# Delta rule on one Trainium2 core: projections from tokens with both norms applied, and other due times

## The chip, the core and the metric

The kernel runs on one core of one Trainium2 chip. The core has four engines that compute, each with its own queue of instructions: TensorE (PE, matrix products, with PEld its weight loads), VectorE (DVE), ScalarE (ACT) and GpSimd (POOL). SyncE (SP) and the others also start DMA transfers. The engines wait for each other through semaphores. PE writes to PSUM, from where DVE or ACT takes the result to SBUF (an "eviction"). The metric is the device time of one execution in microseconds.

## The reference, cut to what matters

Two blocks run one after the other on 512 tokens of width 1024. The first ends in a final RMS norm; the second has a delta-rule layer, a feed-forward layer, a stick-breaking attention and another feed-forward layer. The change lies in the delta-rule layer:

```
x  = first_block(...)                       # its last step: rms_norm with final_norm_g
hn = rms_norm(x, attn_norm)                 # a second norm
proj = hn @ w_in                            # q, k, v, z, b, a
qkv = silu(causal_depthwise_conv(qkv, conv_w))   # four taps along the tokens
q, k = l2_norm(heads(q)), l2_norm(heads(k)); v = heads(v)
beta = sigmoid(b); g = -exp(a_log) * softplus(a + dt_bias)
o = gated_delta_rule(q, k, v, beta, g)      # chunks, a triangular solve each, a scan
out = (rms_norm(o, o_gain) * silu(z)) @ w_out
```

## The kernel before

Activations stand feature by token: a tile of 128 x 512 holds 128 features of all tokens, and eight of them (k = 0 to 7) hold a token's 1024. Each product is made of three matmuls in a rounded format: tokens and weights are each split into a high part (a rounding copy by ACT) and a low part (a subtraction by DVE or POOL). In the traces ah and al are the parts of the tokens, whi and wlo those of the weights, wraw the weights as they come from DRAM, and mm is the PSUM tile of a product. `mm3` issues the three matmuls of 128 x 512.

The order of the instructions of every engine is set when the kernel is built. The code runs through a planner that keeps an estimated clock for each engine. The main line issues the matmuls of the projections; beside it stand "lanes", queues of Python generators with the side products (convolutions, norms, the solve and so on). After each `mm3`, `tick` (line 452) lets a lane take its next step if its due time has come by PE's estimated clock. A generator gives up at each `yield`; `yield 1.5` sets the next step due 1.5 us later than it would be. So due times and changed costs move instructions in the order, and not only in time. Nearly every instruction is recorded at one line, L232, so the rows are told apart by the names of their tiles.

The delta-rule stage is `gdn`. `head`, ahead of it, ends the first block and makes the first projection (key gk, heads 0 and 1) from tokens x * fag, where fag is the product of the two norms' gains; the norms themselves need sums over all 1024 features that are complete only later. `gdn` then makes Rc, the product of both norms' factors for each token (128 x 512, the same on all partitions). Since a factor for each token can be multiplied in behind a projection as well as ahead of it, each projection's PSUM tile is multiplied by Rc as it is evicted.

The projections come in the order `GDN_ORDER`: k0, ba (the columns of beta and g), k1, k2, k3, q0, v0, q1, v1, q2, v2, q3, v3, z0 to z3. `fm_pair` issues one of them: two tiles m = 0, 1, each of eight k, in two halves of the weights, 48 matmuls in all, and calls `ev` for each tile. The steps behind a projection are:

- `conv` evicts to xm: a memset of three columns for the tokens ahead of the first, then `xm = ps * Rc` on DVE. `conv_gen` makes the four taps: ACT multiplies by the last tap's weight, DVE adds three taps (tiles kF, qF or vf, `stt`), ACT applies Silu.
- `norm_gen`, for q and k: ACT squares to cs, PE sums it with ones into the PSUM tile lC, DVE takes that to kss or qss. `v_gen`, for v: PE transposes vf into lC.
- `gates_gen`: from baf (the evicted ba) come beta, then gm, whose parts gmh and gml go to PE (lC<-gm with constants cst, later lB<-ub,gmh).
- `lower` (lB, XTs), DMAs through a scratch tensor scr, then `solve`: thirty pairs of DVE instructions sub and mt, one after the other, which invert the small triangular blocks; then `levels`, `prep`, `scan`, `o_norm` and `fin`, which multiplies with zs.
- z: DVE makes zy = ps * Rc, ACT applies Silu into zs.

Of the kernel before, what the change touches and what calls it, by code (L numbers as in the profile page):

```python
# [12 lines left out]
F = mybir.dt.float32  # L13
FR = mybir.dt.float32r
I32 = mybir.dt.int32
AF = mybir.ActivationFunctionType
OP = mybir.AluOpType
# [3 lines left out]
P = 128  # L21
T = 512
D = 1024
KT = 8
# [76 lines left out]
class Clock:  # L101
# [24 lines left out]
    def tile(s, x):  # L126

        r = s.tiles.get(x.name)
        if r is None:
            r = s.tiles[x.name] = [[], [], 0.0, 0.0]  # L130
            tag = getattr(x, "cap_key", None)
            if tag is not None and x.tag_meta is not None:
                ring = s.rings.setdefault(str(tag), [])
                ring.append(r)
                if len(ring) > x.tag_meta.bufs:
                    r[2] = ring.pop(0)[3]
        return r
# [245 lines left out]
class Kern:  # L383
# [1315 lines left out]
    def gdn(s):  # L1699
        nc, A = s.nc, s.A  # L1700
        V, S, G, PE = nc.vector, nc.scalar, nc.gpsimd, nc.tensor
        tt, stt = V.tensor_tensor, V.scalar_tensor_tensor
# [9 lines left out]
        hh, hl, st1, st2, first = s.begun  # L1712
# [7 lines left out]
        with s.aside():  # L1720
            s.rsqrt_(R1, p1, 1.0 / D)
            tt(out=Rc, in0=R1, in1=R1, op=OP.mult)
            tt(out=Rc, in0=p2, in1=Rc, op=OP.mult)
            s.rsqrt_(Rc, Rc, 1.0 / D)
            tt(out=Rc, in0=Rc, in1=R1, op=OP.mult)

        def scale_gen():
            for k in range(KT):
# [36 lines left out]
        def gates_gen(baf):  # L1765
            ps = bankC([4, 16])
            for t in range(4):
                PE.transpose(ps[:, t], baf[:, t * P:(t + 1) * P], s.ident[0:16, 0:16])
            yield
            S.activation(beta, ps[:, :, 0:8], AF.Exp, scale=-1.0)  # L1770
            V.tensor_scalar(out=beta, in0=beta, scalar1=1.0, scalar2=None, op0=OP.add)
            V.reciprocal(beta, beta)
            tt(out=gm, in0=ps[:, :, 8:16], in1=ab[:, None, 1].to_broadcast([P, 4, 8]), op=OP.add)
            S.activation(gex, gm, AF.Abs)
            S.activation(gex, gex, AF.Exp, scale=-1.0)
            S.activation(gex, gex, AF.Ln, bias=1.0)
            stt(out=gm, in0=gm, scalar=0.0, in1=gex, op0=OP.max, op1=OP.add)
            S.activation(ab[:, 0], ab[:, 0], AF.Exp)
            stt(out=gm, in0=gm, scalar=-1.0, in1=ab[:, None, 0].to_broadcast([P, 4, 8]),
                op0=OP.mult, op1=OP.mult)  # L1780
            s.split(gmh, gml, gm)
            yield
            ps = bankC([4, 32])
            gf = gm.rearrange("p t h -> p (t h)")
            for i, off in enumerate((C_UB, C_CB, C_C0, C_C1)):
                PE.matmul(ps[:, i], s.c[:, off:off + P], gf, start=i == 0, stop=i == 3, skip_group_check=True)
            yield
            V.tensor_copy(gc.rearrange("p t h -> p (t h)"), ps[:, 0])
            tt(out=kds.rearrange("p t h -> p (t h)"), in0=ps[:, 1], in1=gc.rearrange("p t h -> p (t h)"),
               op=OP.subtract)  # L1790
            S.activation(egl.rearrange("p c t h -> p c (t h)"), ps[:, 2:4], AF.Exp)
            S.activation(kds, kds, AF.Exp)
            S.activation(sc1, gc, AF.Exp)
            tt(out=sc1, in0=sc1, in1=beta, op=OP.mult)
            done.add("gates")
            yield

        def conv(ps, m):

            if len(s.lanes["V"]) + len(s.lanes["W"]) > 2:  # L1800
                s.until(lambda: len(s.lanes["V"]) + len(s.lanes["W"]) <= 2)
            xm = tile("xm", [T + 3], bufs=3)
            V.memset(xm[:, 0:3], 0.0)
            tt(out=xm[:, 3:], in0=ps, in1=Rc, op=OP.mult)
            return xm

        def conv_gen(xm, m, y, then):
            w = lambda j: s.vcol("conv_w", 24 * j + m)
            if y is None:
                yield from wait(("v", m - 18))  # L1810
                y = s.tp.tile([P, 512], F, name="vf", tag="nacc", bufs=2)
            S.activation(y, xm[:, 3:], AF.Copy, scale=w(3))
            for j in range(3):
                yield
                stt(out=y, in0=xm[:, j:j + T], scalar=w(j), in1=y, op0=OP.mult, op1=OP.add)
            yield
            S.activation(y, y, AF.Silu)
            yield
            s.add(then(y), "C")


# [1 line left out]
        def norm_gen(x, h, ss):  # L1823
            q = tile("cs", [512])
            S.activation(q, x, AF.Square)
            yield
            p = bankC([4, 2])
            for t in range(4):
                for c in range(2):

                    o = 64 * c if ss is kss else 64 - 64 * c
                    PE.matmul(p[o:o + 64, t], q[:, t * P + 64 * c:t * P + 64 * c + 64], s.ones[:, 0:2],
                              start=t == 0, stop=t == 3, skip_group_check=True)
            yield
            V.tensor_scalar(out=ss[:, :, h], in0=p[:, :, 0], scalar1=EPS, scalar2=None, op0=OP.add)
            if ss is kss:
                done.add(("kss", h))
            hs = slice(h // 4 * 4, h // 4 * 4 + 4)
            if ss is kss and all(("kss", i) in done for i in range(hs.start, hs.stop)):
                S.activation(rho[:, :, hs], kss[:, :, hs], AF.Ln)  # L1840
                S.activation(rho[:, :, hs], rho[:, :, hs], AF.Exp, scale=-0.5)
                V.reciprocal(kss[:, :, hs], kss[:, :, hs])
                tt(out=rho[:, :, hs], in0=rho[:, :, hs], in1=beta[:, :, hs], op=OP.mult)
                yield from wait("gates")
                stt(out=nbeta[:, :, hs], in0=kss[:, :, hs], scalar=-1.0, in1=beta[:, :, hs], op0=OP.mult,
                    op1=OP.mult)
                tt(out=sc1[:, :, hs], in0=sc1[:, :, hs], in1=kss[:, :, hs], op=OP.mult)
                done.add(("k", h // 4))
            if ss is qss:
                V.tensor_scalar(out=ss[:, :, h], in0=ss[:, :, h], scalar1=EPS * P, scalar2=None, op0=OP.mult)  # L1850
                done.add(("q", h))
            yield
# [259 lines left out]
        for key, _, j in s.GDN_ORDER:  # L2112
            if key == "ba":
                beta_and_g()
                continue
            if key == "gk" and j == 1:
                s.add(scale_gen(), "X")
            if key == "gq" and j == 0:
                s.until(lambda: "xd" in done)
                qs.append(s.ap_.tile([P, 8, T], F, name="qF", tag="xT"))  # L2120

            def ev(m, ps, xh):
                h = 2 * j + m
                if key == "gk":
                    x = kF[h // 4][:, h % 4]
                    s.add(conv_gen(conv(ps, 8 + h), 8 + h, x, lambda y: norm_gen(y, h, kss)), "VW"[m])
                elif key == "gq":
                    s.add(conv_gen(conv(ps, h), h, qs[0][:, h], lambda y: norm_gen(y, h, qss)), "VW"[m])
                elif key == "gv":
                    s.add(conv_gen(conv(ps, 16 + h), 16 + h, None, lambda y: v_gen(h, y)), "VW"[m])  # L2130
                elif m == 0:
                    held.append(ps)
                else:
                    g = h // 4
                    if h % 4 == 1:
                        s.until(lambda: (("fin", 0, 3) if g else ("prep", 3)) in done)
                        zs[g] = four("zs", ("kF", "vb")[g])
                        for t in range(4):
                            s.add(fin(g, t), "C")
                    for i, ps in ((h - 1, held.pop()), (h, ps)):  # L2140
                        y = s.tp.tile([P, T + 3], F, name="zy", tag="hF", bufs=2)[:, 0:T]
                        tt(out=y, in0=ps, in1=Rc, op=OP.mult)
                        S.activation(zs[g][:, i % 4], y, AF.Silu)
                    if h % 4 == 3:
                        done.add(("z", g))
            if key == "gk" and j == 0:
                for m in range(2):
                    with s.aside():
                        ev(m, first[m], hh)
                s.tick()  # L2150
                continue
            s.fm_pair(key, parts, ev)
# [328 lines left out]
```

## Time and profile before

| | us |
|---|---|
| three runs | 2069.38, 2071.23, 2073.81 |
| median | 2071.23 |
| profiled run | 2073.48 |
| its span | 2071.5 |

In the profiled run PE is busy for 1972.8 us of the span (95%), DVE for 977.3, ACT for 752.4, POOL for 367.2. The mean granted clock of PE is .966. The delta-rule stage runs from about 660 to 1064 us. A row gives the start and the busy time of an instruction, its engine, operation and tiles, and in brackets how long the engine stood idle before it and which instruction ended that.

### The profile page before, as it was taken

The page shows a single profiled execution, that of the slowest core. Times are in us where ns is not written, and L with a number is a line of the kernel's source. Part 1 is how long each engine was busy: PE and PEld are TensorE (multiplying, and loading weights), DVE is VectorE, ACT ScalarE, POOL GpSimd, SP SyncE. Part 2 cuts the span into 40 slices and gives each one's busy share as a digit, 9 for nine tenths or more (in the row PEclk, how much of TensorE's full clock was granted, in tenths as well). Part 3 has the DMA queues.
Part 4 walks back from the last instruction along what each step waited for, and adds up shares of the span by engine and source line. Part 5 has one row for each costly group of instructions (what it writes and reads, how often), then busy time and mean ns, then how long its engine had stood idle before and what let it go on. Part 6 is the DMA issues. An engine that isn't in the chain of part 4 may idle for free.

```text
span 2071.5 us, 26824 instructions
## 1 busy us (share of the span) xinstructions
PE 1972.8 (95%) x10725; PEld 1479.6 (71%) x10725; DVE 977.3 (47%) x1617; ACT 752.4 (36%) x1184; POOL 367.2 (18%) x292
## 2 busy tenths in 40 slices
PE   7999997999998897999999999999999989999999
PEld 4776765344434776887878888888888868888887
DVE  3544343233345779644364433435666554433432
ACT  3443321322224653433443322224666533222222
POOL 1523101111103442212311100111122211100110
PEclk8998797999999998999999999999999999999999
DMA  8314155999981322210223333223211123333322
GB/s 294 93 45 127 58 187 224 418 415 395 379 313 47 112 72 81 72 30 23 82 72 102 102 100 94 92 92 102 78 62 57 50 71 102 102 94 95 96 92 72
DMA packets 175370, 268.90 MB, mean 130 GB/s; under 512 B 24300, under 2 KB 148456, under 8 KB 162696
## 3 DMA queue, kind: packets, MB, share of 16 engines
q1 hardware_dynamic: 152784, 249.28, 35.1%
q10 hardware_dynamic: 19784, 13.40, 2.3%
q0 software_dynamic: 2672, 4.44, 0.6%
q8 instruction: 87, 1.43, 0.3%
q14 instruction: 43, 0.35, 0.1%
HBM read 263.41 MB, written 7.86 MB: 131 GB/s over the span
## 4 chain that ended last, share of the span: by engine, by line
PE 59%; DVE 6%; ACT 3%; issue 1%; POOL 0%; ACTq 0%; DVEq 0%; POOLq 0%
PE mm L232 50%; PE lA L232 5%; PE lB L232 4%; ACT zm L232 1%; DVE sub L232 1%; DVE kF L232 1%; DVE mt L232 1%; PE lC L232 1%; DVE vf L232 1%; DVE xT L232 1%; DVE al L232 0%; ACT whi L232 0%; ACT ah L232 0%; DVE wlo L232 0%; DVE qF L232 0%
## 5 line engine op out<-in xcount | busy, mean ns | idle before, releaser
L232 PE MATMUL mm<-ah,whi 128*128 128x512 f32 (+1 forms) x1232 | 506.1, 411 | 2.7 <-ACT ah L232 1.2
L232 PE MATMUL mm<-ah,wlo 128*128 128x512 f32 (+1 forms) x1232 | 487.9, 396 | 3.4 <-DVE wlo L232 1.9
L232 PE MATMUL mm<-al,whi 128*128 128x512 f32 (+1 forms) x1232 | 488.2, 396 | 2.7 <-DVE al L232 2.4
L232 DVE TENSOR_TENSOR wlo<-wraw,whi 128x1024 fp32r<-128x1024 f32 (+3 forms) x174 | 216.0, 1242 | 295.1 <-ACT whi L232 295.0
L232 ACT ACTIVATE whi<-wraw 128x1024 fp32r<-128x1024 f32 (+2 forms) x212 | 214.9, 1015 | 334.1 <-PE mm L232 187.0
L232 PEld LDWEIGHTS mm<-ah,whi 128*128 128x128 f32 (+1 forms) x1232 | 234.4, 190 | 62.1 <-issue 7.5
L232 PEld LDWEIGHTS mm<-ah,wlo 128*128 128x128 f32 (+1 forms) x1232 | 234.2, 190 | 57.7 <-DVE wlo L232 3.2
L232 PEld LDWEIGHTS mm<-al,whi 128*128 128x128 f32 (+1 forms) x1232 | 234.8, 191 | 53.3 <-DVE al L232 4.7
L232 POOL TENSOR_TENSOR sg<-sg,fR 128x512 f32<-128x512 f32 x44 | 57.1, 1298 | 526.6 <-ACT sg L232 526.6
L232 PE MATMUL mm<-hidh,whi 128*128 128x512 f32 x352 | 139.2, 395 | 0.0
L232 PE MATMUL mm<-hidh,wlo 128*128 128x512 f32 x352 | 138.0, 392 | 0.0
L232 POOL TENSOR_TENSOR wlo<-wraw,whi 128x1024 fp32r<-128x1024 f32 x38 | 93.3, 2458 | 249.2 <-ACT whi L232 247.7
L232 PE MATMUL mm<-hidl,whi 128*128 128x512 f32 x352 | 136.6, 388 | 0.0
L232 PE MATMUL mm<-slot,moex 128*32 128x512 f32 (+1 forms) x1024 | 122.8, 603 | 0.1
L232 DVE SCALAR_TENSOR_TENSOR xT<-lA,modT,xT 128x512 f32<-128x512 f32 x64 | 48.0, 750 | 107.6 <-PE lA L232 107.6
L232 ACT ACTIVATE moex<-lA,modP,g2P 128x128 f32<-128x128 f32 x64 | 27.5, 455 | 163.6 <-PE lA L232 148.3
L232 PEld LDWEIGHTS mm<-hidh,wlo 128*128 128x128 f32 x352 | 66.1, 188 | 15.5
L232 PEld LDWEIGHTS mm<-hidl,whi 128*128 128x128 f32 x352 | 66.1, 188 | 14.5
L232 PEld LDWEIGHTS mm<-hidh,whi 128*128 128x128 f32 x352 | 66.2, 188 | 13.0
L232 PEld LDWEIGHTS mm<-slot,moex 128*32 128x32 f32 x1024 | 29.0, 110 | 64.1 <-issue 59.2
L232 DVE TENSOR_TENSOR xT<-mm,xT 128x512 f32<-128x512 f32 x64 | 43.9, 687 | 58.0 <-PE mm L232 50.5
L232 ACT ACTIVATE hidh<-fu 128x512 fp32r<-128x512 f32 x44 | 27.8, 633 | 103.9 <-DVE fu L232 103.9
(545 smaller groups left out, 3113.5 us busy)
## 6 DMA issues: line engine op xcount, KB each, us to landing
slot<-in_w_e_in_dram SPq DMA_DIRECT2D x64, 1024.0 KB, 11.9
wraw<-in_w_gu_dram SPq DMA_DIRECT2D x88, 512.0 KB, 3.5
slot<-in_w_e_out_dram SPq DMA_DIRECT2D x32, 1024.0 KB, 13.1
wraw<-in_w_down_dram SPq DMA_DIRECT2D x40, 512.0 KB, 3.4
wraw<-in_w_ada_dram SPq DMA_DIRECT2D x32, 512.0 KB, 4.0
wraw<-in_gdn_w_in_dram SPq DMA_DIRECT2D x32, 512.0 KB, 3.9
wraw<-in_w_kv_dram SPq DMA_DIRECT2D x16, 512.0 KB, 3.3
wraw<-in_w_in_dram SPq DMA_DIRECT2D x14, 512.0 KB, 4.3
```

The lines of the kernel that those rows point to most:

```text
L232: r = f(*a, **k)
```

## The change

A new product fag is made by POOL in `gdn` as well, and a new function `normed` runs right after the projection ba: for each of the eight k, DVE makes hn = x * fag * Rc, ACT rounds it into ah, and DVE subtracts for al. These take the place of the tokens that the first projection used, so all later projections come out of PE with both norms applied. `conv` then has no Rc to multiply with: ACT copies the PSUM tile to xm, except for the first two tiles, which keep the product on DVE. xm has no three columns ahead of it, the memset goes, and each tap covers only the columns that have a token behind them. For z, ACT applies Silu straight from PSUM and zy goes. Three due times are new: 3.0 behind gm and its split, 1.5 behind the Silu of the convolution, 2.0 behind the square of `norm_gen`.

```diff
--- before.py
+++ after.py
@@ -1723,6 +1723,15 @@
             tt(out=Rc, in0=p2, in1=Rc, op=OP.mult)
             s.rsqrt_(Rc, Rc, 1.0 / D)
             tt(out=Rc, in0=Rc, in1=R1, op=OP.mult)
+        fag = tile("fag", [KT])
+        G.tensor_tensor(out=fag, in0=s.vcol("final_norm_g", 0, 8), in1=s.vcol("attn_norm", 0, 8), op=OP.mult)
+
+        def normed():
+
+            for k in range(KT):
+                x = s.tp.tile([P, 512], F, name="hn", tag="nsq", bufs=2)
+                stt(out=x, in0=s.xT[:, k], scalar=fag[:, k:k + 1], in1=Rc, op0=OP.mult, op1=OP.mult)
+                s.split(hh[:, k], hl[:, k], x)
 
         def scale_gen():
             for k in range(KT):
@@ -1779,7 +1788,7 @@
             stt(out=gm, in0=gm, scalar=-1.0, in1=ab[:, None, 0].to_broadcast([P, 4, 8]),
                 op0=OP.mult, op1=OP.mult)
             s.split(gmh, gml, gm)
-            yield
+            yield 3.0
             ps = bankC([4, 32])
             gf = gm.rearrange("p t h -> p (t h)")
             for i, off in enumerate((C_UB, C_CB, C_C0, C_C1)):
@@ -1795,13 +1804,15 @@
             done.add("gates")
             yield
 
-        def conv(ps, m):
+        def conv(ps, m, scale=None):
 
             if len(s.lanes["V"]) + len(s.lanes["W"]) > 2:
                 s.until(lambda: len(s.lanes["V"]) + len(s.lanes["W"]) <= 2)
-            xm = tile("xm", [T + 3], bufs=3)
-            V.memset(xm[:, 0:3], 0.0)
-            tt(out=xm[:, 3:], in0=ps, in1=Rc, op=OP.mult)
+            xm = tile("xm", [T], bufs=3)
+            if scale is None:
+                S.activation(xm, ps, AF.Copy)
+            else:
+                tt(out=xm, in0=ps, in1=scale, op=OP.mult)
             return xm
 
         def conv_gen(xm, m, y, then):
@@ -1809,13 +1820,13 @@
             if y is None:
                 yield from wait(("v", m - 18))
                 y = s.tp.tile([P, 512], F, name="vf", tag="nacc", bufs=2)
-            S.activation(y, xm[:, 3:], AF.Copy, scale=w(3))
+            S.activation(y, xm, AF.Copy, scale=w(3))
             for j in range(3):
                 yield
-                stt(out=y, in0=xm[:, j:j + T], scalar=w(j), in1=y, op0=OP.mult, op1=OP.add)
+                stt(out=y[:, 3 - j:], in0=xm[:, 0:T - 3 + j], scalar=w(j), in1=y[:, 3 - j:], op0=OP.mult, op1=OP.add)
             yield
             S.activation(y, y, AF.Silu)
-            yield
+            yield 1.5
             s.add(then(y), "C")
 
 
@@ -1823,7 +1834,7 @@
         def norm_gen(x, h, ss):
             q = tile("cs", [512])
             S.activation(q, x, AF.Square)
-            yield
+            yield 2.0
             p = bankC([4, 2])
             for t in range(4):
                 for c in range(2):
@@ -2112,6 +2123,8 @@
         for key, _, j in s.GDN_ORDER:
             if key == "ba":
                 beta_and_g()
+                with s.aside():
+                    normed()
                 continue
             if key == "gk" and j == 1:
                 s.add(scale_gen(), "X")
@@ -2119,11 +2132,11 @@
                 s.until(lambda: "xd" in done)
                 qs.append(s.ap_.tile([P, 8, T], F, name="qF", tag="xT"))
 
-            def ev(m, ps, xh):
+            def ev(m, ps, xh, scale=None):
                 h = 2 * j + m
                 if key == "gk":
                     x = kF[h // 4][:, h % 4]
-                    s.add(conv_gen(conv(ps, 8 + h), 8 + h, x, lambda y: norm_gen(y, h, kss)), "VW"[m])
+                    s.add(conv_gen(conv(ps, 8 + h, scale), 8 + h, x, lambda y: norm_gen(y, h, kss)), "VW"[m])
                 elif key == "gq":
                     s.add(conv_gen(conv(ps, h), h, qs[0][:, h], lambda y: norm_gen(y, h, qss)), "VW"[m])
                 elif key == "gv":
@@ -2138,15 +2151,13 @@
                         for t in range(4):
                             s.add(fin(g, t), "C")
                     for i, ps in ((h - 1, held.pop()), (h, ps)):
-                        y = s.tp.tile([P, T + 3], F, name="zy", tag="hF", bufs=2)[:, 0:T]
-                        tt(out=y, in0=ps, in1=Rc, op=OP.mult)
-                        S.activation(zs[g][:, i % 4], y, AF.Silu)
+                        S.activation(zs[g][:, i % 4], ps, AF.Silu)
                     if h % 4 == 3:
                         done.add(("z", g))
             if key == "gk" and j == 0:
                 for m in range(2):
                     with s.aside():
-                        ev(m, first[m], hh)
+                        ev(m, first[m], hh, Rc)
                 s.tick()
                 continue
             s.fm_pair(key, parts, ev)
```

The first place in the order that matters is DVE behind baf. Before:

```order
L232 TENSOR_TENSOR baf<-mm,Rc 16x512
L232 SCALAR_TENSOR_TENSOR kF<-xm,vbT,kF 128x512 x2
L232 TENSOR_SCALAR beta<-beta 128x32
L232 RECIPROCAL beta<-beta 128x32
L232 TENSOR_TENSOR gm<-lC,ab 128x32
```

On DVE at the same place in the changed kernel:

```order
L232 TENSOR_TENSOR baf<-mm,Rc 16x512
L232 SCALAR_TENSOR_TENSOR hn<-xT,fag,Rc 128x512
L232 TENSOR_TENSOR al<-hn,ah 128x512
...
L232 SCALAR_TENSOR_TENSOR kF<-xm,vbT,kF 128x509 x2
L232 TENSOR_SCALAR beta<-beta 128x32
L232 RECIPROCAL beta<-beta 128x32
L232 TENSOR_TENSOR gm<-lC,ab 128x32
```

Eight pairs of hn and al (one is shown) now stand between baf and the first taps. On PE, lC<-gm stood behind 21 of the 48 matmuls of gk1, and now stands behind all 48.

The second place is ACT from the rounding of gm to the square of the norms. The difference, with + for the changed kernel, on ACT's queue:

```order
 L232 ACTIVATE gmh<-gm 128x32
+L232 ACTIVATE whi<-wraw 128x1024
+L232 ACTIVATE xm<-mm 128x512
+L232 ACTIVATE xT<-xT,vaT 128x512
+L232 ACT_TABLE_LOAD
+L232 ACTIVATE kF<-kF 128x512 x2
+L232 ACTIVATE xT<-xT,vaT 128x512
+L219 ACT_TABLE_LOAD
 L232 ACTIVATE egl<-lC 128x64
```

Sixteen instructions stand between gmh and the first cs in the changed kernel, nine before. On PE the first lC<-ones,cs comes 24 matmuls behind lC<-gm, where 33 stood between them before.

The third place is DVE in the solve. Before, these rows are a piece from its middle:

```order
L232 SCALAR_TENSOR_TENSOR qF<-xm,vbT,qF 128x512
L232 MEMSET xm 128x3
L232 TENSOR_TENSOR xm<-mm,Rc 128x512
L232 TENSOR_TENSOR sub<-mt 128x234
L232 TENSOR_TENSOR mt<-mt,sub 128x18x13
```

On DVE the changed kernel has there:

```order
L232 TENSOR_TENSOR mt<-mt,sub 128x19x12
L232 TENSOR_SCALAR qss<-lC 128x4
L232 TENSOR_SCALAR qss<-qss 128x4
L232 SCALAR_TENSOR_TENSOR vf<-xm,vbT,vf 128x509
L232 TENSOR_TENSOR sub<-mt 128x234
L232 TENSOR_TENSOR mt<-mt,sub 128x18x13
```

Between the first sub and the last mt there were 4 xm and 12 taps, and there are now no xm and 7 taps, those of other heads than before. On PE the first matmul of the scan stands 42 matmuls of projections behind the inverses of `levels`, 66 before.

## Rows read from the trace of the kernel before

**Rows 1.** Windows: window, us, busy us (x instructions) by engine, PEclk, DMA share, GB/s.

```profile
691.00:728.00 37.00, 34.24 (x258) 28.34 (x257) 27.05 (x65) 22.33 (x32) 14.56 (x10) 1.00 0.44 134
776.00:821.00 45.00, 34.61 (x159) 27.42 (x158) 43.11 (x89) 11.96 (x17) 13.09 (x6) 0.87 0.25 70
```

**Rows 2.** Waits of PE, 660 to 1064 us: us in total, times, longest.

```profile
PE lC L232 <- ACT cs L232: 10.3, 4, 4.7
PE lC L232 <- DVE gm L232: 3.6, 1, 3.6
...
PE lC L232 <- DVE sub L232: 2.4, 1, 2.4
...
PE lC L232 <- ACT vf L232: 1.8, 2, 1.5
PE lC L232 <- DVE zs L232: 1.7, 1, 1.7
```

**Rows 3.** Timeline of PE: start, us, engine, line, operation, tiles, idle before.

```profile
681.77 1.08 PE L232 MATMUL lC<-gm,cst 128*128 128x32 f32 x8 [3.65 <-DVE gm L232]
682.69 0.70 PE L232 MATMUL mm<-ah,whi 128*128 128x512 f32 x1
...
686.42 0.40 PE L232 MATMUL mm<-ah,whi 128*128 128x512 f32 x1
...
689.20 0.39 PE L232 MATMUL mm<-ah,whi 128*128 128x512 f32 x1
689.42 0.39 PE L232 MATMUL mm<-al,whi 128*128 128x512 f32 x1
...
700.57 0.63 PE L232 MATMUL lC<-ones,cs 128*64 128x2 f32 x16 [2.35 <-ACT cs L232]
```

**Rows 4.** Tiles xm and zy: ns least/median/most, first and last start us, forms.

```profile
L232 DVE TENSOR_TENSOR xm<-mm,Rc x24: 677/691/692, 671.5 to 858.8; 128x512 f32<-128x512 f32 x24
...
L232 DVE TENSOR_TENSOR zy<-mm,Rc x8: 680/684/692, 921.8 to 1022.2; 128x512 f32<-128x512 f32 x8
```

**Rows 5.** Timeline of DVE, around the first projection and behind baf.

```profile
655.75 0.75 DVE L232 SCALAR_TENSOR_TENSOR xT<-lA,modT,xT 128x512 f32<-128x512 f32 x1
657.29 0.75 DVE L232 SCALAR_TENSOR_TENSOR al<-xT,fag,ah 128x512 fp32r<-128x512 f32 x1 [0.79 <-ACT ah L232]
657.96 0.68 DVE L232 TENSOR_TENSOR nacc<-nacc,nsq 128x512 f32<-128x512 f32 x1
...
673.64 2.38 DVE L232 SCALAR_TENSOR_TENSOR kF<-xm,vbT,kF 128x512 f32<-128x512 f32 x1
...
678.74 1.23 DVE L232 TENSOR_SCALAR beta<-beta 128x32 f32<-128x32 f32 x1
...
690.76 0.69 DVE L232 TENSOR_TENSOR xm<-mm,Rc 128x512 f32<-128x512 f32 x1 [2.04 <-PE mm L232]
```

**Rows 6.** Timeline of ACT: a rounding of tokens, and a copy from PSUM.

```profile
656.53 0.72 ACT L232 ACTIVATE ah<-xT,fag 128x512 fp32r<-128x512 f32 x1 [0.95 <-DVE xT L232]
...
839.59 0.60 ACT L232 ACTIVATE XTs<-lB 128x512 f32<-128x512 f32 x1 [0.56 <-PE lB L232]
```

**Rows 7.** Timeline of POOL beside the taps behind baf.

```profile
673.07 5.20 POOL L232 TENSOR_TENSOR wlo<-wraw,whi 128x1024 fp32r<-128x1024 f32 x2 [6.84 <-ACT whi L232]
```

**Rows 8.** Groups of ACT's instructions, 660 to 860 us: busy us, mean ns, idle before.

```profile
L232 ACT ACTIVATE whi<-wraw 128x1024 fp32r<-128x1024 f32 x24 | 25.2, 1051 | 17.2 <-PE mm L232 7.2 <-issue 4.5 <-DVE xm L232 4.1
L219 ACT ACT_TABLE_LOAD x6 | 7.7, 1283 | 0.1
...
L232 ACT ACTIVATE xT<-xT,vaT 128x512 f32<-128x512 f32 x8 | 5.6, 708 | 0.0
```

**Rows 9.** Timeline of DVE in the solve: first sub, a held sub, last mt.

```profile
776.46 0.53 DVE L232 TENSOR_TENSOR sub<-mt 128x30 f32<-128x30 f32 x1
...
782.29 2.55 DVE L232 TENSOR_TENSOR sub<-mt 128x150 f32<-128x150 f32 x1
...
820.02 0.19 DVE L232 TENSOR_TENSOR mt<-mt,sub 128x30 f32<-128x30 f32 x1
```

## The prediction, made before the changed kernel ran

> **What bounds the kernel now.** I read the busy shares first, then the windows of the delta-rule stage, then what PE waits for there, then single instructions. The change reaches no instruction outside that stage (about 660 to 1064 us), so everything else keeps its time. In the stage PE is the bound: between 691 and 728 us it works 34.24 of 37 us at a granted clock of 1.00 [rows 1]. It loses time at a few stops only. From 660 to 1064 us these are 10.3 us for the cs tiles of the norms, 3.6 us for gm, 2.4 us for a sub of the triangular solve, 1.8 us for vf and 1.7 us for zs [rows 2]. A stop costs more than its length: behind the 3.65 us stop for gm, the nine matmuls from 682.69 to 686.42 took 3.73 us [rows 3], where two full-clock matmuls start 0.22 to 0.23 us apart (689.20, 689.42 in [rows 3]), so nine take 2.1 us; a granted half clock adds some 1.6 us. The other weak place is the window 776 to 821 us: DVE works 43.11 of 45 us there, PE 34.61, at a clock of 0.87 [rows 1]. So DVE bounds that one window, and PE the rest. Less work on DVE is worth something only there and at the stops.
>
> **What leaves DVE.** 22 of the 24 xm evictions at 692 ns, 15.2 us, and the 8 zy products, 5.5 us [rows 4]. Of the xm, four lie in the DVE-bound window; the others lie beside a busy PE and their removal shortens nothing by itself. The memsets of three columns and the taps shorter by one to three columns I count at nothing, beside PE's work.
>
> **What is added to the front: S1.** Eight times hn, ah, al, in DVE's queue right behind baf and in ACT's right behind the first two kF, and gk1's 48 matmuls need them in order. The nearest rows are the same three steps on the first projection: the product began at 655.75 [rows 5], its ah at 656.53 [rows 6], its al at 657.29, the next DVE instruction at 657.96 [rows 5]. That is 0.78 + 0.76 + 0.67 = 2.2 us for each k, and 2.1 us if ah without a scale saves 0.1; eight take 16.5 us, because each hn stands behind the previous al and nothing overlaps. PE needs six matmuls for each k, 1.4 us, so it is fed too slowly. The start: baf is done as kF begins at 673.64, and that kF took 2.38 us [rows 5], while POOL worked on wlo, two of them in 5.20 us from 673.07 [rows 7]; a normal one takes 0.75 [rows 5]. The first hn now stands at that place and meets the same wlo, so I add 1.65 us once. The last al then ends near 691.6; the three matmuls of that k and the twelve of the second half (with some of them at the half clock) end gk1 at 695.0. Before, the last evictions of gk1 stood at 690.76 [rows 5].
>
> The work behind the wall is the second cost. Before, two taps, beta and gm stood directly behind baf; beta began at 678.74 [rows 5] and lC<-gm at 681.77 [rows 3], 3.0 us later. That matmul came after 21 matmuls of gk1, with 27 still to do. Now the taps and beta wait for the eighth al, and lC<-gm stands behind all 48. From 691.6: two taps (1.5) of which one is held (1.65, since two whi conversions wait behind the eight ah and POOL's wlo follows them), then the 3.0 us, gives 698.0 rounded up. PE, done at 695.0, stands 3.0 us, the lC take 1.08 [rows 3], and gk2 begins near 699.1, against 690.6 before: 8.5 us; behind the stop come some 1.6 us of half clock: **S1 = +10 us**. Bounds: +5 if nothing is held and the gate is early, +12 if a second hold falls on the hn.
>
> The page "GPSIMD Engine Reference" of the Trainium skill (§ 1. Specifications) says that GpSimd shares its SBUF port with VectorE and that the two contend where a DVE instruction has two SBUF inputs. The 2.38 us kF beside wlo agrees [rows 5, 7], and xm, with one input in PSUM, kept to 0.69 us beside other work [rows 4]. The rule speaks against this change: it trades 22 evictions that cannot be held for 16 instructions, hn and al, that can. By the trace one hold goes into the sum; by the rule alone every later wlo of POOL inside the 16.5 us could add another 1.65 us, and S1 would be nearer +12 than +10.
>
> **What is added to ACT: S2.** ACT gains 8 ah, 22 xm and no zy work. PSUM copies of this size took 0.60 us [rows 6]: 13 us over some 330 us in which ACT has room, 22.33 of 37 us busy in the second window [rows 1]. It matters only in front of an instruction PE waits for. That is the first cs: between gmh and cs there were nine instructions, and there are now sixteen. The added ones are a whi (1.05), two xm (0.60 each), two xT and a kF (0.71 each) and a table load (7.7 us for six) [rows 6, 8], 5.7 us, and the longer chain sums to 11 us. From gmh near 697.5 it reaches the end of cs at 709 to 710.5 with the waits for taps. PE gets there near 706.3: 698.0, the lC of 1.08, 24 matmuls of 0.23 and the 1.6 of half clock. It stands 3 to 4 us and pays the half clock again, some 5.5 us, where before the first stop for a cs was 2.35 us [rows 3]. **S2 = +3** (0 to +5). The due times of 1.5 and 2.0 us cut the later cs stops, of which I count nothing in the stretch of the first queries: **S3 = 0** (-4 to +2).
>
> **The solve: S4.** It begins later by S1, S2 and its place in the order, near 793 instead of 776.46, where its first sub stood behind an xm. Before, it ended at 820.02 [rows 9], with 4 xm and 12 taps between its 60 instructions. Now there are 7 taps and no xm: 43.11 us less 4 x 0.69 less 5 x 0.75 is some 36 us, less again if fewer subs are held as the one of 2.55 us was [rows 9]; the end comes at 825 to 829. PE, pushed back 11.5 us, no longer stands where it did, but the lC of the last v heads wait for taps in the chain, some 10 us in all against 2.4 for sub and 1.8 for vf [rows 2] and the long tail of waits before. Of the 11.5 us, 4 are given back: **S4 = -4**, from -16 (all of the 10.4 us that PE did not work in this window, 45 less 34.61, and the 5.9 us of half clock that 0.87 means over 45 us [rows 1]) to +2.
>
> **The end: S5.** The 1.7 us stop for zs [rows 2] goes, since ACT reads PSUM itself and one lC, not two, stands at the last place: **-1.7** (-3 to 0). POOL's product fag is 8 columns wide and nobody waits for it early: nothing.
>
> Sum: 10 + 3 + 0 - 4 - 1.7 = **+7.3**. The profiled run of before took 2073.48 us, 2.25 above the median of 2071.23. Against the median that is 2071.23 + 7.3 = **2078.5 us**.
>
> **Rivals.** *A, the forecast:* PE is starved behind baf and only part comes back. For it: three steps with no overlap at 2.1 us a k against 1.4 us of PE. Against it: the stage has many stops that may vanish. Chance 0.50.
> *B, faster:* one mechanism, the DVE-bound window opens. The solve has 36 us of work instead of 43 and the evictions no longer wait in DVE's queue, so PE never stops from 776 to 821: S4 is -16 instead of -4, and 7.3 - 12 = -4.7, 2066.5 us. It decides if the lC of the v heads find their taps done, that is, if the solve ends before PE comes to them. Against it: it also begins 16 us later. Chance 0.26.
> *C, even:* half of that window comes back, S4 = -11: 2071.5 us. Chance 0.21.
> *D, slower still:* the solve's delay goes through the block inverses into the scan, whose start stands 42 instead of 66 matmuls behind; 24 matmuls of cover at 0.23 us are 5.6 us, and a stop of that size plus its half clock gives 2078.5 + 7 = 2085.5. It is inside A's side; chance 0.03 as a case of its own.
> That the change does not do what it says is ruled out by the order of the instructions: the hn stand in it, and the xm stand on ACT.
>
> **How the numbers follow.** 0.2% is 4.1 us, about what a measurement of this kernel can tell from no change: faster is below 2067.1, slower above 2075.4. A and D give slower 0.53; B gives faster 0.25 and C, with the edge of B, 0.22. The range reaches from B's 2066.5 less 2.5 for a smaller S1, 2064, to D's 2085.5 plus the upper bounds of S1 and S2 in part, 2089. The likeliest case has 2074 to 2085 as its own.
>
> **What would show it.** S1: eight hn and al in a row behind baf, a period of 2.1 us, PE stopping at gk1 and again at lC<-gm, gk2 beginning near 699. If the hn run in under 1.5 us each, S1 is wrong. S2: a stop of 3 us or more at the first cs. S4: the last mt of the solve at 825 to 829, and waits of PE for vf of some 10 us; if PE waits under 3 us there, B holds. S5: no stop for zs. A much longer wait at the scan would be D.

## The result and the profile after

The changed kernel takes 2083.18 us (median of five runs, 2082.54 to 2089.28), the kernel before 2071.23. The ratio is 1.0060, with a 95% interval from 1.0042 to 1.0078: slower by 8.7 to 16 us. The profiled run of after took 2082.65 us with a span of 2080.8; that is 9.3 us more span than before.

The waits of PE from 660 to 1080 us, after (us in total, times, longest), answer to [rows 2]:

```profile
PE lC L232 <- DVE vb L232: 6.8, 1, 6.8
PE lC L232 <- ACT cs L232: 6.8, 3, 3.3
PE lC L232 <- DVE qss L232: 4.8, 1, 4.8
PE mm L232 <- ACT ah L232: 3.4, 3, 3.1
PE lA L232 <- POOL gS L232: 3.1, 1, 3.1
PE lC L232 <- DVE gm L232: 2.9, 1, 2.9
PE mm L232 <- DVE al L232: 2.5, 3, 2.1
PE mm L232 <- ACT mh L232: 1.8, 1, 1.8
```

The stops for cs fell from 10.3 to 6.8 us, and those for sub, vf and zs are gone. New are vb (6.8), qss (4.8) and, behind baf, the longest of ah (3.1). The stop for gm is shorter but stands elsewhere. The stop for gS stood in the kernel before too, and was as long there (3.1). DVE behind baf, after, answers to [rows 5]:

```profile
672.86 0.68 DVE L232 TENSOR_TENSOR baf<-mm,Rc 16x512 f32<-16x512 f32 x1 [0.92 <-PE mm L232]
673.47 1.69 DVE L232 SCALAR_TENSOR_TENSOR hn<-xT,fag,Rc 128x512 f32<-128x512 f32 x1
675.92 0.69 DVE L232 TENSOR_TENSOR al<-hn,ah 128x512 fp32r<-128x512 f32 x1 [0.76 <-ACT ah L232]
676.53 0.74 DVE L232 SCALAR_TENSOR_TENSOR hn<-xT,fag,Rc 128x512 f32<-128x512 f32 x1
678.03 0.69 DVE L232 TENSOR_TENSOR al<-hn,ah 128x512 fp32r<-128x512 f32 x1 [0.76 <-ACT ah L232]
...
690.69 0.69 DVE L232 TENSOR_TENSOR al<-hn,ah 128x512 fp32r<-128x512 f32 x1 [0.76 <-ACT ah L232]
691.30 3.54 DVE L232 SCALAR_TENSOR_TENSOR kF<-xm,vbT,kF 128x509 f32<-128x509 f32 x2
694.77 1.23 DVE L232 TENSOR_SCALAR beta<-beta 128x32 f32<-128x32 f32 x1
```

One al begins 2.11 us behind the other (675.92, 678.03), with DVE idle for 0.76 us in each period. The eighth al ends at 691.38; only then come the taps and beta. On PE, answering to [rows 3], the first matmul of gk1, then lC<-gm, the first of gk2, and the first lC<-ones,cs:

```profile
675.94 0.50 PE L232 MATMUL mm<-ah,whi 128*128 128x512 f32 x1 [3.11 <-ACT ah L232]
...
697.80 1.89 PE L232 MATMUL lC<-gm,cst 128*128 128x32 f32 x8 [2.92 <-DVE gm L232]
699.51 0.77 PE L232 MATMUL mm<-ah,whi 128*128 128x512 f32 x1
...
710.91 0.63 PE L232 MATMUL lC<-ones,cs 128*64 128x2 f32 x16 [3.27 <-ACT cs L232]
```

lC<-gm stands 24.9 us behind the start of baf; before it was 681.77 less 672.83, 8.9 us. Two windows of after, in the columns of [rows 1]:

```profile
673.00:718.00 45.00, 33.65 (x115) 23.73 (x115) 31.76 (x39) 23.30 (x40) 16.89 (x10) 0.77 0.17 47
679.00:685.00 6.00, 5.67 (x11) 2.97 (x12) 3.73 (x7) 1.89 (x3) 0.00 (x0) 0.50 0.00 0
```

and the first of them in the kernel before:

```profile
673.00:718.00 45.00, 38.59 (x237) 30.95 (x235) 30.89 (x60) 27.60 (x46) 23.91 (x13) 0.96 0.36 111
```

PE has 115 instructions in this window instead of 237. Its granted clock is 0.77 against 0.96. From 679 to 685 us it is 0.50, that is 1.2 GHz, although PE counts as busy for 5.67 of 6 us. Ahead of that PE had stood 3.11 us for the first ah, until 675.94; behind the stop it got 3 matmuls in each period of hn, ah, al.

### The profile page after: what moved, and what is told of

Its sections match the earlier page's. It is cut to its first block, busy times and chain, and to the rows that moved or that the text cites. A ratio compares the mean times of both kernels' runs of the same rounds, so it can differ in the third digit from the quotient of the medians.

```text
span 2080.8 us, 26825 instructions
## 1 busy us (share of the span) xinstructions
PE 1975.8 (95%) x10725; PEld 1478.5 (71%) x10725; DVE 971.8 (47%) x1579; ACT 770.2 (37%) x1216; POOL 368.3 (18%) x293
## 3 DMA queue, kind: packets, MB, share of 16 engines
q1 hardware_dynamic: 152784, 249.28, 34.7%
## 4 chain that ended last, share of the span: by engine, by line
PE 52%; ACT 2%; DVE 1%; issue 0%; POOL 0%; POOLq 0%; ACTq 0%
PE mm L232 46%; PE lA L232 4%; PE lB L232 2%; ACT zm L232 1%; DVE xT L232 0%; ACT whi L232 0%; DVE wlo L232 0%; DVE ml L232 0%; DVE sqT L232 0%; ACT ah L232 0%; DVE al L232 0%; PE lC L232 0%; ACT nsq L232 0%; POOL wlo L232 0%; DVE E L232 0%
## 5 line engine op out<-in xcount | busy, mean ns | idle before, releaser
L232 PEld LDWEIGHTS mm<-hidh,whi 128*128 128x128 f32 x352 | 66.1, 188 | 13.7
L232 PEld LDWEIGHTS mm<-hidl,whi 128*128 128x128 f32 x352 | 66.1, 188 | 13.5
```

The lines of the kernel that those rows point to most:

```text
L232: r = f(*a, **k)
```

## Experiments

Three theories stood at first: the chain of hn, ah, al is the loss (theory 1); the evictions by ACT are (theory 2); the due times are (theory 3). The rival of all three, that the order of the instructions late in the stage decides by itself, came up on the way. In the table, gm is the start of lC<-gm behind the start of baf, q1 the start of q1's second eviction behind it, and the rest the time from there to the end of the span, all from one profiled run of each. Two runs of one kernel may differ by several us (the run with evictions by DVE took 2066.72 to 2076.86), so the ratio, from ten runs or so, is the verdict on the time, and the columns tell where it lies. How many side products PE has done by q1 differs a little among the orders, so a us or two between the last columns says nothing. Nor does one trace carry a few microseconds: baf itself begins between 671.5 and 677.94 us, and the time behind the last lC<-cst,vb, at the end of the stage, is between 1015.6 and 1020.1 us, though the kernels hardly differ in either place. Some profiled runs lie far from the median of their ten: chain only at 2073.29 (median 2079.22), after with the old due times at 2073.00 (2077.17), chain from k2 at 2072.67 (2076.79), due times alone at 2074.20 (2069.89). Each ratio is to runs of the kernel before that were taken beside it, with medians of 2071.23 to 2073.86 us, so a ratio and a time in us can tell a little differently.

| kernel | ratio to before, 95% interval | gm | q1 | rest |
|---|---|---|---|---|
| before | 1 | 8.9 | 103.0 | 1295.7 |
| after | 1.0060, 1.0042 to 1.0078 | 24.9 | 116.1 | 1291.8 |
| after without the chain | 0.9972, 0.9956 to 0.9988 | 9.0 | 97.3 | 1293.9 |
| the same, old due times | 0.9994, 0.9979 to 1.0009 | 8.9 | 101.1 | 1291.3 |
| due times alone | 0.9988, 0.9971 to 1.0005 | 9.0 | 102.8 | 1291.3 |
| hn one ahead | 1.0025, 1.0012 to 1.0038 | 19.2 | 110.6 | 1291.0 |
| chain from k2 | 1.0015, 0.9999 to 1.0031 | 8.7 | 113.7 | 1285.7 |
| chain during k1 | 1.0056, 1.0039 to 1.0072 | 7.2 | 111.0 | 1293.5 |
| evictions by DVE | 0.9999, 0.9981 to 1.0016 | 25.3 | 117.3 | 1278.6 |
| after, old due times | 1.0021, 1.0007 to 1.0035 | 25.3 | 114.2 | 1284.9 |
| chain only | 1.0025, 1.0006 to 1.0044 | 24.8 | 117.0 | 1280.3 |
| after, state zeroed by DVE | 1.0040, 1.0022 to 1.0058 | 24.8 | 115.8 | 1289.0 |
| after, one due time 1.25 | 1.0043, 1.0024 to 1.0063 | 24.9 | 116.2 | 1287.0 |
| due times, state zeroed by DVE | 0.9986, 0.9966 to 1.0007 | 9.0 | 102.8 | 1289.9 |

### Without the chain

```diff
-                with s.aside():
-                    normed()
```

> The changed kernel without the eight hn, ah, al: later projections take the tokens of the first one, so the factor of each token is left out of k1 to z3 and the result is not the reference's. Everything else of the change stays (evictions by ACT, short taps, due times). Theory 1, the chain of hn, ah, al behind baf is the loss: lC<-gm goes back from 697.8 to about 681 us, gk2 begins near 691, and the time falls by 10 us or more, to 2067 to 2073 us. Theory 2, the evictions by ACT and its longer queue are the loss: the stops for cs stay and the time stays above 2078. Theory 3, the new due times are the loss: also above 2078.

Measured: ratio 0.9972, and 0.88% below the changed kernel (0.9972 against 1.0060), 18 us (15 us between the medians). In the trace q1 comes 18.8 us earlier behind baf and the rest is 2.1 us longer, so the gain lies where the chain was. lC<-gm went back to 9.0 us behind baf, and the clock of the front returned:

```profile
673.00:718.00 45.00, 40.91 (x228) 32.46 (x227) 34.76 (x35) 30.94 (x52) 24.93 (x13) 0.96 0.33 100
```

The time is 2068.57 us, within what theory 1 had. So with the eight steps left out, and with all evictions by ACT and all due times in place, the change is 0.3% faster than before instead of 0.6% slower. The same with the old due times:

```diff
-            yield 3.0
+            yield
-            yield 1.5
+            yield
-            yield 2.0
+            yield
```

> The changed kernel without the eight hn, ah, al and with the old due times: what is left of the change is the eviction by ACT without a multiplication, the shorter taps and z by ACT alone (the factor of each token is left out of k1 to z3, so the result is not the reference's). If the evictions are worth something by themselves: 0.1 to 0.3% faster than before. If the gain of the run without the chain came from the due times alone: within 0.1% of before.

Ratio 0.9994, the second of the two cases: no gain that can be told from none. What the evictions free on DVE is worth little alone.

### The due times alone

The same three lines the other way round, put into the kernel before.

> The kernel before with the three new due times alone (3.0 behind gm, 1.5 behind Silu, 2.0 behind the square). Theory 1 and 2: within 3 us of 2071, either way, with the stops for cs shorter than 10.3 us in all. Theory 3: slower than 2076.

Ratio 0.9988 (2069.89 us), interval across 1: theory 3 falls as a cause in itself, since no cost of them alone shows. The shorter stops for cs did not come: in the trace they are 13.7 us in all instead of 10.3.

### A shorter chain

hn of k + 1 is issued ahead of al of k.

```diff
+            ahead = []
+            for k in range(KT + 1):
+                if k < KT:
                     x = s.tp.tile([P, 512], F, name="hn", tag="nsq", bufs=2)
                     stt(out=x, in0=s.xT[:, k], scalar=fag[:, k:k + 1], in1=Rc,
                         op0=OP.mult, op1=OP.mult)
-                s.split(hh[:, k], hl[:, k], x)
+                    ahead.append(x)
+                if k:
+                    s.split(hh[:, k - 1], hl[:, k - 1], ahead[k - 1])
```

> The changed kernel with hn of k+1 ahead of al of k in DVE's queue, so that ACT's ah lies beside DVE's next hn. Same instructions, same work. Theory 1: the period falls from 2.11 us to 1.4 us, the last al ends near 686 instead of 691.4, lC<-gm comes near 693 instead of 697.8, and the time falls by 4 to 6 us, to 2077 to 2079. Theory 2 and 3: the chain gets shorter but the time stays within 2 us of 2083.

DVE in this run:

```profile
680.39 0.75 DVE L232 SCALAR_TENSOR_TENSOR hn<-xT,fag,Rc 128x512 f32<-128x512 f32 x1
681.06 0.68 DVE L232 TENSOR_TENSOR al<-hn,ah 128x512 fp32r<-128x512 f32 x1
681.78 0.75 DVE L232 SCALAR_TENSOR_TENSOR hn<-xT,fag,Rc 128x512 f32<-128x512 f32 x1
682.45 0.68 DVE L232 TENSOR_TENSOR al<-hn,ah 128x512 fp32r<-128x512 f32 x1
```

The period is 1.39 us (681.06 to 682.45), lC<-gm came 5.7 us earlier behind baf (19.2 against 24.9), q1 5.5 us earlier. The time is 2079.62 us and the ratio 1.0025, 0.35% below that of the changed kernel: 7 us by the ratios and 3.6 between the medians, where theory 1 had 4 to 6.

### The chain moved away from the gate

First in pairs: gk1 keeps the old tokens and Rc, and the rewriting is issued between gk1's groups of matmuls and behind them.

```diff
-                with s.aside():
-                    normed()
...
+            if key == "gk" and j == 1:
+                s.fm_pair(key, parts, lambda m, ps, xh: ev(m, ps, xh, Rc), beside=normed())
```

> The changed kernel with the eight steps one projection later: gk1 still takes the old tokens and is evicted by DVE with Rc, beta and gm stand in front, and the tokens are rewritten in pairs while gk1's second half and gk2's first half run. The projections gk2 to z3 and their evictions by ACT are as in the changed kernel; one more DVE copy keeps the second norm's factor. Theory 1: lC<-gm stands near 682 again, PE is fed without a stop beyond 1 us at gk2, and the time is 2066 to 2073 us. Theory 2: the ACT queue is as full as before, above 2078. A result between, 2073 to 2078, would say that the eight steps cost also where PE has other work.

The time is 2076.79 us and the ratio 1.0015, the result between the two theories: the eight steps cost here too. lC<-gm is back at 8.7 us, yet q1 is only 2.4 us earlier. The wait moved to gk2:

```profile
688.39 0.80 PE L232 MATMUL mm<-ah,whi 128*128 128x512 f32 x1 [4.31 <-ACT ah L232]
694.84 0.72 PE L232 MATMUL mm<-ah,whi 128*128 128x512 f32 x1 [3.22 <-ACT ah L232]
```

The first hn stood in DVE's queue behind four taps and an xm, and the later ones behind a second xm and POOL's scaling of xT. Then finer, right behind each last reading matmul, with the scaling of xT one projection later. In this version the lanes take no step during the second tile of gk1 (`tick` is left out there), so the taps can't either:

```diff
+                        if after and m:
+                            after(k, c)
...
-            if key == "gk" and j == 1:
+            if key == "gk" and j == 2:
                 s.add(scale_gen(), "X")
```

> A version meant to keep both sides: gk1 takes the old tokens and is evicted with Rc; each hn, ah, al is put right behind the last matmul of gk1 that reads the old token tile, with the next hn ahead of al, so that half of the steps lie beside gk1's second half and half beside gk2's first half; the scaling of xT for the residual starts one projection later and needs no second factor. Theory 1: lC<-gm stays 9 us behind baf, PE stops for ah and al no longer than 2 us in all at gk2, and the time comes near the kernel without the chain, 2066 to 2071 us. If the taps that the steps push back make the first cs late instead, a stop of 4 us or more stands there and the time is 2072 to 2077.

This was the worst of the variants, 1.0056. PE is fed at gk2, but one stop replaces the others:

```profile
701.72 0.49 PE L232 MATMUL lC<-ones,cs 128*64 128x2 f32 x6 [12.00 <-DVE kF L232]
```

Its row names a tap kF, but the cs that the matmul reads is done only at 701.66 as well, just ahead of the start. The taps for it are done on DVE at 692.34; ACT then makes two ah, the Silu, two more ah and a whi, among others, before it:

```profile
697.40 1.15 ACT L232 ACTIVATE kF<-kF 128x512 f32<-128x512 f32 x2
...
701.05 0.61 ACT L232 ACTIVATE cs<-kF 128x512 f32<-128x512 f32 x1
```

I had expected 4 us or more there as the bad case, and 2072 to 2077 us; it was 12.00 us, and 2082.72. The sixteen DVE instructions of the chain take some 11.5 us (8 x 0.74 + 8 x 0.69), and in all three places that were tried PE waited, for the chain itself or for something behind it on DVE or ACT.

### Evictions by DVE, and the old due times

```diff
-                S.activation(xm, ps, AF.Copy)
+                V.tensor_copy(out=xm, in_=ps)
```

> The changed kernel with the 22 xm copies out of PSUM made by DVE instead of ACT (z stays with ACT). The chain of hn, ah, al and the due times stay. Theory 1, the chain ahead of gk1 is the loss: lC<-gm stays about 25 us behind baf and the time stays between 2080 and 2090 us (over 0.3% slower than before); since the eviction by ACT is a small gain, it is a few us slower than the changed kernel. Theory 2, ACT's evictions are the loss: the time falls to 2075 or less.

By the time alone theory 2 was right and theory 1 wrong: 0.9999, as fast as before. The trace says otherwise about the place. lC<-gm (25.3) and q1 (117.3) are as late as in the changed kernel. The whole gain is in the rest, 1278.6 against 1291.8 us. The stretch of the scan, from the start of the last xm to the last lC<-cst,vb, first of before, then of after, then of this run:

```profile
858.80:1052.20 193.40, 185.35 (x1155) 156.21 (x1155) 87.20 (x193) 73.92 (x123) 42.09 (x27) 0.95 0.16 47
```

```profile
881.60:1063.70 182.10, 175.69 (x1104) 147.47 (x1102) 79.57 (x180) 76.74 (x125) 41.74 (x26) 0.97 0.16 50
```

```profile
884.50:1056.10 171.60, 171.60 (x1115) 145.12 (x1115) 79.83 (x183) 73.28 (x121) 41.56 (x26) 1.00 0.18 53
```

PE stands still for 6.4 us there after (182.10 less 175.69), and the clock of 0.97 is worth some 5 us more; with evictions by DVE it neither stands nor slows. So 10.5 of the 13.2 us lie here. Since no xm is evicted any more in this stretch, the eviction by ACT can't cost there by itself; that the order of the scan's steps among the z projections makes the difference is argued, and only one of the stops was tested (below).

> The changed kernel with the three due times as they were before. Theory 1: the chain stays, and the time is that of the changed kernel plus what the due times give by themselves (0 to 5 us in the run of them alone), so 2082 to 2090 us. Theory 3, the due times cost in the presence of the chain, though not alone: below 2080.

Below 2080, so by the bound I had set theory 3 held here: 1.0021. The due times that cost nothing alone cost 0.39% in the presence of the chain (1.0060 less 1.0021). In the traces q1 has 1.9 us of this and the rest 6.9 us. How the due times make the rest longer stays open.

> The chain of hn, ah, al with evictions of xm by DVE and the old due times: of the change only the normed tokens, the shorter taps and z by ACT alone are left. If the chain costs some 13 us up to the end of q1 and nothing gives it back: 2080 to 2088. If the later stretch takes up a delay of the front whenever DVE evicts, as in the run with evictions by DVE: 2070 to 2076. In both lC<-gm is 25 us behind baf.

1.0025 (2079.22 us): between the two cases. The front is as late (117.0), and in the profiled run, 5.9 us below the median, the scan runs without a stop: from 900 to 1065 us PE is busy for 164.79 of 165 us.

```profile
900.00:1065.00 165.00, 164.79 (x1039) 138.27 (x1038) 81.10 (x175) 70.91 (x115) 38.14 (x24) 1.00 0.19 58
```

### How much the order alone can do

```diff
-            yield 1.5
+            yield 1.25
```

> The changed kernel with the due time behind Silu 1.25 instead of 1.5 us: the work and ACT's order are the same and PE's order differs in a few places. It shows how far a small change of order moves the time by itself. If the order hardly matters: within 2 us of 2083. If single undone parts gained 5 to 12 us by new places in the order: a shift of 3 us or more either way, with the front up to q1 unchanged.

The front is the same to 0.1 us (24.9, 116.2). In the solve's stretch (790 to 860 us) the stop for vb fell from 6.8 to 2.7 us:

```profile
PE lC L232 <- DVE qss L232: 4.8, 1, 4.8
PE lC L232 <- DVE vb L232: 2.7, 1, 2.7
PE lC L232 <- ACT cs L232: 2.2, 1, 2.2
PE lC L232 <- ACT vf L232: 1.2, 1, 1.2
```

In DVE's queue vb now begins at 830.02, ahead of the last two pairs of the solve, and no longer behind them. The rest is 4.8 us shorter in the trace, 3.3 of them up to the last lC<-cst,vb. The time is 2080.43 us, 2.75 us lower, between the two cases, and the ratio is 0.17% lower with intervals that overlap. So a quarter of a microsecond in one due time shortens a stop by 4 us in the trace; that the time follows is not shown.

```diff
-                G.memset(states[g], 0.0)
+                V.memset(states[g], 0.0)
```

> The changed kernel with one edit: the zeroing of the scan's state gS is done by DVE instead of POOL. In the trace of the changed kernel this memset of 0.53 us stands in POOL's queue behind a wlo of 2.34 us, PE waits 3.10 us for it, and a half clock follows. The run with evictions by DVE made its 12 us in this stretch, where it has no such stop. Theory A, the order in the scan and not the eviction made that run's gain: the 3.10 us stop and its half clock go, 3 to 7 us faster than the changed kernel, 2076 to 2080. Theory B, the eviction by ACT itself costs: no more than 2 us.

The stop of 3.1 us for gS on POOL is gone from the waits (900 to 1065 us):

```profile
PE lA L232 <- DVE gS L232: 1.5, 1, 1.5
PE lB L232 <- DVE kd L232: 1.5, 1, 1.5
```

The stage is 3.1 us shorter in the trace, no more; the time is 2080.99 us, 2.2 us lower, between the two theories, and the ratio is 0.20% lower, with intervals that overlap. The half clock behind the stop (960.7 to 967.5 us after) is gone as well, but one as long has come behind the stop of 1.5 us for kd (929.2 to 936.1). So theory A holds, in the trace, for the length of this one stop only. What makes the rest of the gain of the run with evictions by DVE stays open.

> The kernel before with the three new due times and with the scan's state zeroed by DVE: no chain, evictions by DVE with Rc. If the due times are worth the 2.5 us of their own run and the 3.10 us stop for gS and its clock go: 2062 to 2068, faster than both kernels. If the stop only moves to the next late step of the scan: as the due times alone, 2068 to 2072.

0.9986, from 0.9966 to 1.0007: not clear of no change, and the expected 2062 to 2068 was not reached (2071.08); it is the second case, as the due times alone. No version was shown to beat the kernel before while computing the same.

## Why the prediction was right, point by point

**S1** was right in nearly every number: a period of 2.11 us (forecast 2.1), the eighth al ending at 691.38 (691.6), lC<-gm at 697.80 (698.0) with a stop of 2.92 us (3.0), gk2's first matmul at 699.51 (699.1). The first hn was held as forecast, though by less: 1.69 us for a normal 0.74, so 0.95 instead of 1.65. The two taps behind the chain took 3.54 us for a normal 1.5, so 2.0 instead of 1.65. Both lie beside a wlo on POOL:

```profile
672.27 2.35 POOL L232 TENSOR_TENSOR wlo<-wraw,whi 128x1024 fp32r<-128x1024 f32 x1 [7.23 <-ACT whi L232]
691.68 2.62 POOL L232 TENSOR_TENSOR wlo<-wraw,whi 128x1024 fp32r<-128x1024 f32 x1 [17.07 <-ACT whi L232]
```

The held hn ends at 675.16 and POOL's wlo at 674.62; the taps end at 694.84 and POOL's wlo at 694.30. No other hn or al was held, since POOL had no wlo between the two. The Trainium skill's "GPSIMD Engine Reference", § 1. Specifications, says that GpSimd's SBUF interfaces are shared with VectorE, with contention where a DVE instruction has two SBUF inputs. Both rows agree with it; for a second hold inside the chain, which by that rule alone would have brought S1 near +12, there was no wlo.

**S2** was right in size by the stop (3.27 us for 3 to 4), a little late (PE reached it at 707.64 instead of 706.3). What the sum had wrong is the way: I charged 1.6 us of half clock behind gm and 1.6 behind cs. In the trace there is more of it, behind the stops for the first ah, for gm and for cs:

```profile
677.40:687.60 10.20, 9.74 (x22) 5.90 (x23) 6.55 (x10) 3.12 (x5) 0.00 (x0) 0.50 0.04 15
697.90:704.70 6.80, 6.80 (x20) 5.72 (x21) 6.27 (x7) 4.72 (x8) 4.43 (x2) 0.50 0.25 63
711.50:714.90 3.40, 3.40 (x10) 2.72 (x9) 3.33 (x4) 1.28 (x2) 1.73 (x2) 0.50 0.53 151
```

At half the clock these cost up to 5.1, 3.4 and 1.7 us. What the first is worth by itself is not known, since DVE and ACT set the end of the chain. **S1, S2 and S3** were forecast at 13 + 0 (S4 goes on with 11.5, which the sum does not give); the second eviction of q1 is 13.1 us later behind baf. From baf to there, before and after:

```profile
672.83:775.86 103.03, 94.70 (x597) 77.35 (x596) 76.14 (x161) 57.53 (x87) 46.42 (x25) 0.97 0.33 93
672.86:788.94 116.08, 102.62 (x597) 81.60 (x598) 81.19 (x154) 66.51 (x103) 41.79 (x22) 0.91 0.28 82
```

PE has 597 instructions in both. It stands still for 13.5 us instead of 8.3, and the clock of 0.91 instead of 0.97 is worth some 7 us more: by this count the larger part of the 13.1 us is half clock. The 22.33 of 37 us that S2 reads for ACT are those of the first window of [rows 1]; in the second, ACT works 11.96 of 45 us, so it has room there all the more.

**S4** is the term that was mis-sized. The solve took 34.7 us (forecast 36 or less), but began at 797.74 instead of near 793 and ended here:

```profile
832.42 0.19 DVE L232 TENSOR_TENSOR mt<-mt,sub 128x30 f32<-128x30 f32 x1
```

that is 3 to 7 us later than the 825 to 829 of the forecast. PE then stood 6.8 us for vb, 4.8 us for qss and 2.0 us for cs in this stretch, where I had some 10 us in all. The mechanism was in part another: no stop was for the taps of vf. The longest stands at a v head, but for vb, which comes right behind the solve's last mt in DVE's queue:

```profile
832.57 0.65 DVE L232 TENSOR_TENSOR vb<-lC,rho 128x512 f32<-128x512 f32 x1
```

From q1 to the last lC<-cst,vb the lag fell from 13.1 to 11.5 us. These 1.6 us are no more than the stop for zs (S5), so S4 gave back nothing, instead of 4 us.

**S5** was right: no stop for zs. Before, it stood ahead of the last lC<-cst,vb:

```profile
1051.86 0.63 PE L232 MATMUL lC<-cst,vb 128*128 128x128 f32 x4 [1.66 <-DVE zs L232]
```

Behind this lC the lag fell by another 2.2 us to the end of the span. No term of the forecast has these, and the stretch varies by 4.5 us among the traces (1015.6 to 1020.1 us).

The sum in the trace is 13.1 - 1.6 - 2.2 = 9.3 us for the forecast 7.3; the two profiled runs lie 9.2 us apart. The remaining 2.8 us of the 12.0 between the medians come from the step to the median: the profiled run of before lay 2.25 us above its median, and that of after 0.5 us below its own.

Of the rivals, B found its condition nowhere in the changed kernel: PE did stop at the v heads, for longer than 3 us. Its cause, DVE freed of evictions, brought no gain of 12 us even without the chain. D did not come: the longest stop of the scan, for gS, is 3.1 us as before. C did not come either: of the 11 us that it gives back by the solve, nothing came.

What the forecast did not contain: the time behind q1 swings by 13 us among kernels with nearly the same front (1278.6 to 1291.8), and the ratios of the two ends, 0.9999 and 1.0060, are about as far apart. The changed kernel lies at the slow end of that. S4 was put at -4 between -16 and +2, and the 4 us that it did not give back were in part made up by 2.2 us that no term has; that the total came out this near was in part luck.

## What to carry to other kernels

A preparatory step with three instructions on two engines, run once at the head of a projection, cost its full latency here, where PE needs it in order; price the period (product, rounding, subtraction) against PE's time for the same slice, and issue the next product ahead of the last subtraction. Look at what stands behind such a block on the same queue: moving it by up to one projection moved the stop from gm to ah or to cs and saved 0.45% in one version and nothing that shows in the other. When an edit moves a planned order, compare the front of the traces landmark by landmark before giving a total time to a part: undoing one part gained as much as 0.6% here at a place that it does not touch.

## What was not expected of the hardware

PE's granted clock stayed at half for much longer than the stop ahead of it. Behind the stop of 3.11 us for the first ah it was 0.50 from 677.4 to 687.6 us, 10.2 us, where the matmuls came three at a time at first; the five other runs with the period of 2.11 us have 10.2 us there too. With hn one ahead, a period of 1.39 us and a stop of 2.93 us, it was 3.4 us:

```profile
681.50:684.90 3.40, 3.40 (x8) 2.13 (x9) 3.29 (x6) 1.63 (x3) 0.00 (x0) 0.50 0.03 9
```

Before, behind the stop of 3.65 us for gm, it was 3.4 us as well (682.8 to 686.2). The feeding can't be all of it: behind the stop of 2.92 us for gm, after, it was 6.8 us, with PE busy all the time. What sets the length is not shown here. In the run without the chain, which has no such stop, the six microseconds from 679 to 685 have a clock of 1.00:

```profile
679.00:685.00 6.00, 5.73 (x29) 4.60 (x29) 4.74 (x10) 3.35 (x8) 2.92 (x2) 1.00 0.37 108
```

PE is busy for about the same share as in the changed kernel (5.67 of 6 us), but with 29 instructions against 11; the busy share hides the clock, the count shows it. ACT's copy of 128 x 512 from PSUM took 0.60 us in the median of 22, close to the row from which it was priced.

```profile
L232 ACT ACTIVATE xm<-mm x22: 572/598/604, 698.9 to 881.6; 128x512 f32<-128x512 f32 x22
```
